# Gates between the pairs of a recurrence, prompt scores on quarter tiles, and later side work in a planned transformer layer

## The chip, the cores and the metric

The kernel runs on one core of one Trainium2 chip. The metric is the time of one execution in device microseconds. A difference is measured by running the two kernels in turn on the same chip. Names used below: PE is the matrix engine (TensorE), DVE the vector engine, ACT the scalar engine, POOL the general engine (GpSimd), SP the engine that issues most DMAs. "Records" are instructions as the profile counts them: an f32 matmul leaves two, an fp32r matmul one.

## The reference, cut to what matters

One layer over 640 tokens (512 prompt tokens and 8 x 16 sample tokens), width 1024, all in f32:

```python
x += 0.5 * swiglu(rms_norm(x), w_ffn1_up, w_ffn1_down)      # d_ff = 2816
h  = rms_norm(x); P = h @ w_in                              # q, k, v, four HGRN blocks, two LRU blocks, 3 gates
A  = sliding-window attention, 16 query heads, 4 key heads of 64, chunks of 64 that see 3 chunks of keys,
     q and k normalised per head, softmax with a learned sink per head
B  = HGRN2: gated linear recurrence with a 128x128 state per head, 8 heads
C  = causal convolution (4 taps), then RG-LRU (a scan over time), times gelu(gate branch)
x += (sig(gA) * A @ w_attn_o + sig(gB) * B @ w_hgrn_o + sig(gC) * C @ w_lru_o) @ w_out
x += 0.5 * swiglu(rms_norm(x), w_ffn2_up, w_ffn2_down)
```

## The kernel before

All activations lie transposed, 128 features on the partitions and the 640 tokens along the row. A projection, `proj`, is one 128-column block of a weight matrix against all tokens: the block is loaded into `wr`, split into a rounded high half `wh` (a cast, L750) and a low half `wl` (a subtraction on DVE, L751), and multiplied in fp32r as three products (`wh` with the high and the low half of the tokens, `wl` with the high half), in two halves of 320 tokens in two banks of the tag `pp` (four banks). With K = 1024 that is 48 matmuls of 320 columns. `halves` pairs the two banks with the halves of a destination. `scaled` empties them while multiplying by `RS`, the row norm's factor per token; with `late` it copies first and multiplies afterwards in one product of 640. `parts` splits a result into high (ACT) and low (DVE) halves for a following projection.

From the fifth FFN block on, `pair` computes a gate block and an up block together from seven products instead of eight (a Strassen form), which needs sums and differences of the normalised tokens. `combos` makes these: a first part at once, and a second part, `rest()`, before the first down projections. `CHUNKS` cuts the 22 FFN blocks in four groups (4, 6, 6, 6), each followed by eight down projections.

In attention, `query(m)` normalises two query heads (one block of 128 features). For the prompt it used to be written into `qb` as a block diagonal (`qb` is 1024 wide, half of it zeros), so that one matmul of K = 128, M = 128 gives the scores of both heads for one chunk of 64 queries. `prompt(m, g, qb)` goes through the chunks in two halves `hh` of four chunks; each half has two score operations, one for each bank `ps` of the tag `me` (two banks in all), each followed by the maximum, the exponentials and the division, then transposes and, by `pv_of`, the product with the values. `sample` does the same for the sample tokens, `merge` multiplies by the output weights and the gates. `AHEAD` tells how many gate projections are put behind each query block.

The LRU, `lru()`, goes through eight feature blocks in four pairs. For a pair: the convolution (DVE), the two small gate matrices (into `me`), exponentials and square roots on ACT, the scan (L1227), and the projections LG with gelu, product and `parts`. After all four pairs five gate projections (`gate(GC, m, "mgC")`) and the first HGRN head's projections follow, then `merge`. The last columns of the convolution and of the scan are copied into `CB` for the outputs.

The order of instructions is not written by hand. Every operation goes into `Sched` with a cost for each engine that may do it, its reads and writes, and a priority: the running number of the projection (`S.item`), plus `S.late`, or minus a `lag` for preparation that may come earlier. `Sched.run` plays the program through with these costs: again and again it takes the operation that can start first, among those within 0.04 us the one of lowest priority, and so fixes each engine's order. Buffers of one tag (and so the banks of `pp` and `me`) are given out in program order. On the chip each engine then follows its fixed order and waits on semaphores. Costs are formulas such as these:

```python
def dve(n, f, aps=0):
    return ("DVE", 0.066 + 1.042e-3 * n + 0.063 * aps, f)
...
return {32: 0.021 + 0.415e-3 * m.n, 64: max(0.112, 0.93e-3 * m.n)}.get(w, max(0.216, 0.011 + m.n / 600.0))
```

Of the kernel before, what the change touches and what calls it, by code (L numbers as in the profile page):

```python
# [16 lines left out]
P = 128  # L17
TP = 512
# [327 lines left out]
def trunk_kernel(ctx: ExitStack, tc: tile.TileContext, A: dict, O: list):  # L346
# [122 lines left out]
    SK = fixed("SK", [P, 32])  # L469
    NAR = 13864  # L470
# [52 lines left out]
    in_region(RW, 2, [("qb", 1024, 2), ("pw", 1024, 2)])  # L523
# [367 lines left out]
    def ffn(wu, wd, norm, R, H, sfx, done, aside=()):  # L891
        ops = None
        for f0, nf in CHUNKS:
            for f in range(nf):
# [16 lines left out]
            if f0 == 0:  # L911
                rest()
            for m in range(KD):
# [58 lines left out]
    def attention():  # L972
        ck, cv = A["cache_attn_k"][0], A["cache_attn_v"][0]
        sk = A["attn_sinks"][0].rearrange("(m two) -> two m", two=2)
        for h in range(2):
            dma(SK[h * 64:h * 64 + 64, 0:8].at(h), sk[h:h + 1, :].to_broadcast([64, 8]), after=(PRM.v,), small=True)
            for b in range(4):
                p0 = b * 32 + h * 16
                dma(SK[p0:p0 + 16, 8:16].at((b, h)), sk[h:h + 1, :].to_broadcast([16, 8]), after=(PRM.v,), small=True)
        S.op([dve(16, lambda: nc.vector.tensor_scalar(SK[:, 16:32](), SK[:, 0:16](), -1.0, None, op0=ALU.mult))], [SK.v, RS.v], [SK.v])  # L980
# [13 lines left out]
        for b in qbs + qss + pws:  # L994
            fill(b.v, 0.0, only=("POOL",))

        def qknorm(ps):
            q, s, r, u = scaled("qq", ps), S.buf("qt"), S.buf("qr"), S.buf("qu")
# [5 lines left out]
        for j in range(2):  # L1004
            q, r = qknorm(proj(W, 0, KD, AK + j * P, RA))
# [35 lines left out]
        def prompt(m, g, qb):  # L1041
            pT = S.buf("pT")
            for hh in range(2):
# [4 lines left out]
                for i in range(2):  # L1048
                    ps = S.buf("me")
                    calls = []  # L1050
                    for c in (2 * i, 2 * i + 1):
                        n = hh * 4 + c
                        w = min(n + 1, 3) * 64
                        o = (c % 2) * 192
                        e = 192 if c % 2 == 0 else 256
                        win[c] = ps[:, o:o + w], pw3[:, c, e - w:e].at(c)
                        calls.append((win[c][0], qb[:, n * P:(n + 1) * P], kd[g][:, (n + 1) * 64 - w:(n + 1) * 64], True, True))
                    mm(calls)
                    if hh == 0 and i == 0:
                        red = [(mx[:, c:c + 1].at(i), win[c][0]) for c in range(2)]  # L1060
# [5 lines left out]
                    ts(mi, mi, -0.125, ALU.mult, SK[:, 16 + m:17 + m], ALU.min, only=("DVE",))  # L1066
                    fn(ei, mi, AF.Exp, bias=SK[:, m:m + 1])
                    for c in (2 * i, 2 * i + 1):
                        fn(win[c][1], win[c][0], AF.Exp, scale=0.125, bias=mx[:, c:c + 1].at(i), accum=den[:, c:c + 1].at(i))
                    tt(di, di, ei, ALU.add, only=("DVE",))  # L1070
                    recip(di, di)
                    for c in (2 * i, 2 * i + 1):
                        ts(win[c][1], win[c][1], den[:, c:c + 1].at(i), ALU.mult)
# [8 lines left out]
            def pv_of(k, n):  # L1082

                src = pT[:, k * 512:k * 512 + n * 256].r("p (c h q) -> p c h q", h=2, q=64)
                mm([(po[h * 64:h * 64 + 64, k * P:(k + n) * P].r("p (c q) -> p c q", q=64), V[:, k, g, :], src[:, :, h, :], k == 0, k == 3)
                    for h in range(2)])
# [82 lines left out]
    def lru():  # L1169
        bds = [S.buf("bd") for _ in range(2)]  # L1170
        for b in bds:
            fill(b.v, 0.0)
        for j in range(4):
            xcs, rs, igs, las, lts = [], [], [], [], []
            for i in range(2):
# [16 lines left out]
                cp(CB[:, m, 0:3].at(m), y[:, TP - 3:TP], only=("POOL", "DVE"))  # L1192
                cp(CB[:, m, 3:27].at(m).r("p (b j) -> p b j", b=NB), smp(y.v)[:, :, SB - 3:], only=("POOL", "DVE"))
# [22 lines left out]
            for i in range(2):  # L1216
# [10 lines left out]
                S.op([dve(T, lambda o=hs.v, a=a.v, t=t.v: nc.vector.tensor_tensor_scan(o(), a(), t(), 0.0, op0=ALU.mult, op1=ALU.add))],  # L1227
                     [a.v, t.v], [hs.v])
                cp(CB[:, m, 27:28].at(m), hs[:, TP - 1:TP], only=("POOL", "DVE"))
                cp(CB[:, m, 28:36].at(m), smp(hs.v)[:, :, SB - 1], only=("POOL", "DVE"))  # L1230
                hss.append(hs)
            for i in range(2):
# [4 lines left out]
                parts(RB, m, g.v)  # L1237
        co = S.buf("co")
# [8 lines left out]
        more = lambda m: gate(GC, m, "mgC")  # L1247
        gates = [more(m) for m in range(5)]
# [7 lines left out]
    def hgrn():  # L1256
# [44 lines left out]
        def head(i):  # L1301
# [31 lines left out]
            for h in (2, 4, 8, 16, 32, 64):  # L1333
# [4 lines left out]
                if h < 32:  # L1338
# [149 lines left out]
```

## Time and profile before

| | us |
|---|---|
| median of three runs | 1921.0 (1920.73 to 1923.34) |
| the profiled execution, its own time | 1923.28 |
| span of the profile, first to last instruction | 1921.5 |
| PE busy | 1898.9 (99%) |
| DVE busy | 1389.1 (72%) |
| ACT busy | 735.8 (38%) |
| POOL busy | 44.3 (2%) |
| mean granted clock of PE | 0.996 |

Roughly, FFN1 ends near 460 us, attention runs from there to 712, its merge to 767, the LRU from 767 to 892, gates, LRU merge and HGRN to 1340, HGRN's merge and `w_out` to 1480, FFN2 to the end. Busy times are unions of the instructions' intervals; a matmul's interval is longer than the distance to the next, since matmuls overlap, so distances from start to start are used for what PE's work costs. Idle time of an engine counts only where PE waits for it. In a row of the timeline the square brackets give the engine's idle time before the row and what ended it.

### The profile page before, as it was taken

To read this page: it belongs to the slowest core of one execution; us is meant where nothing else is said; L and a number is where in the kernel's file an instruction comes from. 1 tells how busy PE (TensorE), PEld (TensorE's weight loads), DVE (VectorE), ACT (ScalarE), POOL (GpSimd) and SP (SyncE) were. 2 spreads that over 40 slices of the span, in tenths; PEclk is the share of its full clock that TensorE was granted. 3 is DMA by queue.
4 is the path that set the end of the run, shared out by engine and by line. 5 is a ranking of instruction groups with operands and counts; after the bars stand their busy time and mean duration, and the time that the engine had idled before them with its cause. 6 is when DMAs were issued, how large, how long until landed. Compare 5 with 4: busy or idle time off the path is not lost.

```text
span 1921.5 us, 35215 instructions
## 1 busy us (share of the span) xinstructions
PE 1898.9 (99%) x14654; PEld 1853.0 (96%) x14654; DVE 1389.1 (72%) x2599; ACT 735.8 (38%) x1295; POOL 44.3 (2%) x86
## 2 busy tenths in 40 slices
PE   8999999999999999999999999999999999999999
PEld 8999999999999999999999999999999999999998
DVE  7897685877787773787547778877556978586784
ACT  6343251433478630876002344335112324142340
POOL 2000000000000000020000000000000000000000
PEclk9999999999999999999999999999999999999999
DMA  6232332224321212213222222222322133222322
GB/s 144 66 94 80 93 87 78 75 78 139 102 62 50 62 48 77 61 57 103 77 77 74 84 80 79 79 81 83 122 72 77 56 99 90 87 65 79 99 64 80
DMA packets 303488, 156.89 MB, mean 82 GB/s; under 512 B 21324, under 2 KB 300956, under 8 KB 303328
## 3 DMA queue, kind: packets, MB, share of 16 engines
q1 hardware_dynamic: 302576, 154.58, 27.7%
q8 instruction: 115, 1.88, 0.4%
q0 software_dynamic: 736, 0.06, 0.4%
q14 instruction: 45, 0.37, 0.1%
q10 hardware_dynamic: 16, 0.00, 0.0%
HBM read 143.32 MB, written 10.63 MB: 80 GB/s over the span
## 4 chain that ended last, share of the span: by engine, by line
PE 93%; DVE 4%; ACT 2%; issue 1%; DMA 1%; SPq 0%; ACTq 0%; DVEq 0%
PE pp L438 84%; PE me L438 4%; PE ml L438 3%; PE ml L447 1%; PE me L447 1%; DVE AR L383 1%; ACT AR L393 1%; DVE AR L369 1%; DVE RB L369 0%; DVE AR L1227 0%; ACT L393 0%; DMA RX<-in_x_prompt_dram 0%; DVE wl L751 0%; SPq L417 0%; DVE RA L369 0%
## 5 line engine op out<-in xcount | busy, mean ns | idle before, releaser
L438 PE MATMUL pp<-RA,wh 128*128 128x320 f32 x4192 | 815.0, 314 | 0.3 <-DVE AR L369 0.3
L438 PEld LDWEIGHTS pp<-RA,wh 128*128 128x128 f32 x4192 | 659.1, 189 | 13.1 <-issue 9.7
L438 PE MATMUL pp<-RA,wl 128*128 128x320 f32 x2096 | 490.7, 310 | 4.9 <-DVE wl L751 4.9
L438 PE MATMUL pp<-RB,wh 128*128 128x320 f32 x2016 | 389.0, 310 | 0.9 <-DVE AR L369 0.9
L438 PEld LDWEIGHTS pp<-RA,wl 128*128 128x128 f32 x2096 | 354.7, 188 | 5.9 <-DVE wl L751 5.9
L438 PEld LDWEIGHTS pp<-RB,wh 128*128 128x128 f32 x2016 | 320.4, 188 | 1.5 <-DVE AR L369 1.4
L750 DVE CAST wh<-wr 128x1024 fp32r<-128x1024 f32 (+2 forms) x142 | 89.4, 630 | 237.2 <-PE pp L438 236.5
L438 PE MATMUL pp<-RB,wl 128*128 128x320 f32 x1008 | 241.9, 310 | 1.6 <-DVE wl L751 1.6
L751 DVE TENSOR_TENSOR wl<-wr,wh 128x1024 fp32r<-128x1024 f32 (+2 forms) x196 | 216.7, 1106 | 1.6 <-ACT wh L750 1.0
L836 ACT CAST RW<-AR 128x512 fp32r<-128x512 f32 x180 | 110.4, 621 | 264.9 <-PE pp L438 135.0
L438 PEld LDWEIGHTS pp<-RB,wl 128*128 128x128 f32 x1008 | 172.1, 188 | 1.9 <-DVE wl L751 1.9
L369 DVE TENSOR_TENSOR AR<-AR 128x640 f32<-128x640 f32 (+12 forms) x272 | 140.0, 519 | 28.9 <-ACT AR L393 16.5
L369 DVE TENSOR_TENSOR AR<-pp,AR 128x320 f32<-128x320 f32 x268 | 127.6, 485 | 35.8 <-PE pp L438 32.7
L393 ACT ACTIVATE AR<-AR 128x640 f32<-128x640 f32 (+2 forms) x184 | 110.5, 604 | 96.9 <-DVE AR L369 89.6
L438 PE MATMUL pp<-RX,RW 128*128 128x320 f32 x864 | 138.6, 309 | 0.0
L438 PEld LDWEIGHTS pp<-RX,RW 128*128 128x128 f32 x864 | 129.6, 188 | 0.0
L833 DVE TENSOR_TENSOR RW<-AR,RW 128x512 fp32r<-128x512 f32 x180 | 122.3, 686 | 2.4 <-ACT RW L836 0.9
L393 ACT ACT_TABLE_LOAD x73 | 93.7, 1283 | 2.5 <-PEq L1476 1.4
L402 ACT COPY AR<-me 128x512 f32<-128x512 f32 (+3 forms) x72 | 25.8, 373 | 123.9 <-PE me L447 115.2
L383 DVE SCALAR_TENSOR_TENSOR AR<-pp,AR 128x320 f32<-128x320 f32 x128 | 61.3, 483 | 15.5 <-PE pp L438 15.4
L438 PE MATMUL pp<-RY,RW 128*128 128x320 f32 x432 | 69.2, 309 | 0.0
L750 ACT CAST wh<-wr 128x1024 fp32r<-128x1024 f32 (+1 forms) x54 | 53.7, 994 | 36.9 <-PE pp L438 36.5
(195 smaller groups left out, 1960.7 us busy)
## 6 DMA issues: line engine op xcount, KB each, us to landing
wr<-in_w_in_dram SPq DMA_DIRECT2D x84, 512.0 KB, 3.7
wr<-in_w_ffn_up_dram SPq DMA_DIRECT2D x52, 512.0 KB, 3.8
AR<-in_w_ffn_up_dram SPq DMA_DIRECT2D x36, 512.0 KB, 4.6
wr<-in_w_ffn_down_dram SPq DMA_DIRECT2D x48, 384.0 KB, 3.3
wr<-in_w_ffn_down_dram SPq DMA_DIRECT2D x16, 256.0 KB, 2.8
wr<-in_w_attn_o_dram SPq DMA_DIRECT2D x8, 512.0 KB, 3.7
AR<-in_state_hgrn_dram SPq DMA_DIRECT2D x8, 512.0 KB, 4.7
wr<-in_w_lru_o_dram SPq DMA_DIRECT2D x8, 512.0 KB, 3.8
```

Of the source, the lines that this page charges most:

```text
L369: alts = [dve(out.n, lambda: nc.vector.tensor_tensor(out(), a(), b(), op=op))]
L383: return S.op([dve(out.n, lambda: nc.vector.scalar_tensor_tensor(out(), a(), ap_of(s), b(), op0=op0, op1=op1), isinstance(s, View))], [a, ...
L393: nc.scalar.activation(out(), a(), func, bias=ap_of(bias), scale=ap_of(scale), **kw)
L402: alts = [act(out.n, lambda: nc.scalar.copy(out(), a()), 0, a), dve(out.n * (1.0 if a.in_psum else 0.5), lambda: nc.vector.tensor_copy(out ...
L438: nc.tensor.matmul(o(), l(), m(), start=s, stop=e)
L447: nc.tensor.transpose(o(), i(), d())
L750: S.op([act(nk * P, lambda: nc.scalar.copy(h(), r())), dve(nk * P * 0.5, lambda: nc.vector.tensor_copy(h(), r()))], [r], [h], lag=2)
L751: S.op([dve(nk * P, lambda: nc.vector.tensor_tensor(l(), r(), h().bitcast(F32), op=ALU.subtract))], [r, h], [l], lag=1.5)
L833: S.op([dve(out.n, lambda: nc.vector.tensor_tensor(out(), a(), b(), op=op))], [a, b], [out], lag=lag)
L836: S.op([act(out.n, lambda: nc.scalar.copy(out(), a()))], [a], [out], lag=lag)
```

## The change

Six edits, and all orders are planned anew.

1. `rest()` gets `S.late = 4.0`, so its operations rank four projections later.
2. In FFN2 the first block's two projections, and in attention the two key projections, use `late` scaling.
3. Prompt scores: `qb` becomes 512 wide without zeros and is written by one product. Each half `hh` has one score operation with eight matmuls of K = 64, M = 64: for each chunk `c` and head `f` the query's 64 features on partitions `b`, the result on partitions `a`. For odd chunks the heads change places in the result, and even chunks go to one `me` bank, odd ones to the other; both banks are taken by the one operation. The sinks SK get eight columns in the changed order, and `pv_of` picks the columns in the changed order.
4. In the LRU a gate projection comes between the two LG projections of each pair.
5. The scan's planned cost goes from `T` to `2 * T`, and a K = 64, M = 64 matmul gets a planned cost of its own.
6. The small copies into `CB`, and those into `hatt` in HGRN, may no longer go to POOL; they go to ACT or DVE.

```diff
+            if l.proto.shape[0] == 64 and w == 64:
+                return max(0.054, 0.42e-3 * m.n)
...
-    in_region(RW, 2, [("qb", 1024, 2), ("pw", 1024, 2)])
+    in_region(RW, 2, [("qb", 512, 2), ("pw", 1024, 2)])
...
-                    late = not sfx and f < 2
+                    late = f < (1 if sfx else 2)
...
             if f0 == 0:
+                S.late = 4.0
                 rest()
+                S.late = 0.0
...
+            dma(SK[64 - h * 64:128 - h * 64, 32:40].at((h, 8)), sk[h:h + 1, :].to_broadcast([64, 8]), after=(PRM.v,), small=True)
...
-            q, r = qknorm(proj(W, 0, KD, AK + j * P, RA))
+            q, r = qknorm(proj(W, 0, KD, AK + j * P, RA), True)
...
-                for i in range(2):
-                    ps = S.buf("me")
-                    calls = []
-                    for c in (2 * i, 2 * i + 1):
...
-                        calls.append((win[c][0], qb[:, n * P:(n + 1) * P], kd[g][:, (n + 1) * 64 - w:(n + 1) * 64], True, True))
-                    mm(calls)
+                pss, calls = [S.buf("me") for _ in range(2)], []
+                for c in range(4):
...
+                    win[c] = pss[c % 2][:, o:o + w], pw3[:, c, e - w:e].at(c)
+                    for f in range(2):
+                        a, b = f * 64, (f ^ (c % 2)) * 64
+                        calls.append((win[c][0][a:a + 64, :], qb[b:b + 64, n * 64:(n + 1) * 64], kd[g][b:b + 64, (n + 1) * 64 - w:(n + 1) * 64],
+                                      True, True))
+                mm(calls)
...
+            stt(qb.v, q[:, 0:TP], prm(QN), r[:, 0:TP], ALU.mult, ALU.mult)
             for h in range(2):
                 a, b = h * 64, h * 64 + 64
-                stt(qb[a:b, :].at(h).r("p (n h q) -> p n h q", n=8, h=2)[:, :, h, :], q[a:b, 0:TP].r("p (n q) -> p n q", n=8), prm(QN, a, b),
-                    r[a:b, 0:TP].r("p (n q) -> p n q", n=8), ALU.mult, ALU.mult)
...
+        gates, more = [], lambda m: gate(GC, m, "mgC")
...
-                cp(CB[:, m, 0:3].at(m), y[:, TP - 3:TP], only=("POOL", "DVE"))
+                cp(CB[:, m, 0:3].at(m), y[:, TP - 3:TP], only=("ACT", "DVE"))
...
-                S.op([dve(T, lambda o=hs.v, a=a.v, t=t.v: nc.vector.tensor_tensor_scan(o(), a(), t(), 0.0, op0=ALU.mult, op1=ALU.add))],
+                S.op([dve(2 * T, lambda o=hs.v, a=a.v, t=t.v: nc.vector.tensor_tensor_scan(o(), a(), t(), 0.0, op0=ALU.mult, op1=ALU.add))],
...
+                if i == 0:
+                    gates.append(more(len(gates)))
...
-        gates = [more(m) for m in range(5)]
+        while len(gates) < 5:
+            gates.append(more(len(gates)))
...
-                            cp(a4[p, :, p].at(j), atc[p, :].r("p (t l) -> p t l", t=NT), only=("ACT", "POOL"))
+                            cp(a4[p, :, p].at(j), atc[p, :].r("p (t l) -> p t l", t=NT), only=("ACT", "DVE"))
```

More of the change, by code (lines that the diff above doesn't have):

```diff
@@ L468, in trunk_kernel @@
     CB = fixed("CB", [P, KD, 36])
-    SK = fixed("SK", [P, 32])
-    NAR = 13864
+    SK = fixed("SK", [P, 48])
+    NAR = 13824
     AR = sb("AR", [P, NAR])
@@ L993, in attention, with qknorm @@
         qbs, qss, pws = ([S.buf(t) for _ in range(2)] for t in ("qb", "qs", "pw"))
-        for b in qbs + qss + pws:
+        for b in qss + pws:
             fill(b.v, 0.0, only=("POOL",))
-        def qknorm(ps):
-            q, s, r, u = scaled("qq", ps), S.buf("qt"), S.buf("qr"), S.buf("qu")
+        def qknorm(ps, late=False):
+            q, s, r, u = scaled("qq", ps, late), S.buf("qt"), S.buf("qr"), S.buf("qu")
             rnorm(q, s, r, u, bd64, 64)
@@ L1047, in prompt @@
                 win = {}
[L1048 to L1060 removed]
+                pss, calls = [S.buf("me") for _ in range(2)], []
+                for c in range(4):
+                    n = hh * 4 + c
+                    w = min(n + 1, 3) * 64
+                    o = (c // 2) * 192
+                    e = 192 if c % 2 == 0 else 256
+                    win[c] = pss[c % 2][:, o:o + w], pw3[:, c, e - w:e].at(c)
[4 more added lines that the diff above has]
+                mm(calls)
+                for i, ps in enumerate(pss):
+                    cols = [(2 * i, win[i]), (2 * i + 1, win[i + 2])]
+                    if hh == 0:
+                        red = [(mx[:, c:c + 1].at(i), v[0]) for c, v in cols]
                     else:
@@ L1065, in prompt @@
                     mi, di, ei = (x[:, 2 * i:2 * i + 2].at(i) for x in (mx, den, es))
[L1066 to L1069, printed above, removed]
+                    pos, neg = ((0, 16), (32, 40))[i]
+                    ts(mi, mi, -0.125, ALU.mult, SK[:, neg + m:neg + m + 1], ALU.min, only=("DVE",))
+                    fn(ei, mi, AF.Exp, bias=SK[:, pos + m:pos + m + 1])
+                    for c, v in cols:
+                        fn(v[1], v[0], AF.Exp, scale=0.125, bias=mx[:, c:c + 1].at(i), accum=den[:, c:c + 1].at(i))
                     tt(di, di, ei, ALU.add, only=("DVE",))
                     recip(di, di)
-                    for c in (2 * i, 2 * i + 1):
-                        ts(win[c][1], win[c][1], den[:, c:c + 1].at(i), ALU.mult)
+                    for c, v in cols:
+                        ts(v[1], v[1], den[:, c:c + 1].at(i), ALU.mult)
                 for i in range(2):
@@ L1191, in lru @@
                     stt(smp(xc.v)[:, :, :s], hist, w, smp(xc.v)[:, :, :s], ALU.mult, ALU.add)
-                cp(CB[:, m, 0:3].at(m), y[:, TP - 3:TP], only=("POOL", "DVE"))
-                cp(CB[:, m, 3:27].at(m).r("p (b j) -> p b j", b=NB), smp(y.v)[:, :, SB - 3:], only=("POOL", "DVE"))
+                cp(CB[:, m, 0:3].at(m), y[:, TP - 3:TP], only=("ACT", "DVE"))
+                cp(CB[:, m, 3:27].at(m).r("p (b j) -> p b j", b=NB), smp(y.v)[:, :, SB - 3:], only=("ACT", "DVE"))
                 r, ig = S.buf("lr"), S.buf("li")
@@ L1226, in lru @@
                 hs = rs[i]
-                S.op([dve(T, lambda o=hs.v, a=a.v, t=t.v: nc.vector.tensor_tensor_scan(o(), a(), t(), 0.0, op0=ALU.mult, op1=ALU.add))],
+                S.op([dve(2 * T, lambda o=hs.v, a=a.v, t=t.v: nc.vector.tensor_tensor_scan(o(), a(), t(), 0.0, op0=ALU.mult, op1=ALU.add))],
                      [a.v, t.v], [hs.v])
-                cp(CB[:, m, 27:28].at(m), hs[:, TP - 1:TP], only=("POOL", "DVE"))
-                cp(CB[:, m, 28:36].at(m), smp(hs.v)[:, :, SB - 1], only=("POOL", "DVE"))
+                cp(CB[:, m, 27:28].at(m), hs[:, TP - 1:TP], only=("ACT", "DVE"))
+                cp(CB[:, m, 28:36].at(m), smp(hs.v)[:, :, SB - 1], only=("ACT", "DVE"))
                 hss.append(hs)
@@ L1246, in lru @@
         dma(O[11], co[28:36, :])
-        more = lambda m: gate(GC, m, "mgC")
-        gates = [more(m) for m in range(5)]
+        while len(gates) < 5:
+            gates.append(more(len(gates)))
         pre.append(heads(0))
```

10 lines of the change are left out of this document (6 added, 4 removed).

## The prediction

> **What bounds the kernel now.** I read the page first, then who TensorE (PE) waits for, then busy times by stretch, then the timeline at each place where PE stands still.
>
> ```profile
> PE 1898.9 (99%) x14654; PEld 1853.0 (96%) x14654; DVE 1389.1 (72%) x2599; ACT 735.8 (38%) x1295; POOL 44.3 (2%) x86
> ```
>
> PE is busy 99% of the span, so only two things can pay: less PE work, or the little that PE stands still or runs slowly. The list of PE's own waits shows how little that is (total us, times, longest):
>
> ```profile
> PE pp L438 <- DVE wl L751: 6.4, 5, 2.4
> PE me L447 <- DMA RX<-in_x_prompt_dram: 4.6, 2, 2.6
> ```
>
> The DMA line is the start, which the change leaves alone. The other is VectorE (DVE) being late with the low half `wl` of a weight block. What follows such a gap costs too. Busy times by stretch (PE, PEld, DVE, ACT, POOL with counts; granted clock, DMA share, GB/s):
>
> ```profile
> 1340.00:1480.00 140.00, 140.00 (x957) 140.00 (x956) 80.94 (x116) 24.70 (x34) 0.00 (x0) 1.00 0.31 95
> ```
> ```profile
> 76.00:86.00 10.00, 8.41 (x46) 7.99 (x45) 9.11 (x21) 3.15 (x5) 0.00 (x0) 0.83 0.19 54
> 780.00:802.00 22.00, 19.22 (x110) 18.33 (x109) 19.73 (x38) 18.07 (x25) 3.72 (x4) 0.84 0.18 53
> 820.00:834.00 14.00, 11.57 (x77) 11.04 (x76) 14.00 (x29) 5.19 (x7) 4.05 (x6) 1.00 0.26 75
> 862.00:868.00 6.00, 5.55 (x35) 4.87 (x34) 6.00 (x14) 2.62 (x4) 2.63 (x3) 1.00 0.23 68
> 1486.00:1492.00 6.00, 5.11 (x33) 4.63 (x32) 4.55 (x8) 0.74 (x1) 0.00 (x0) 1.00 0.00 0
> 1532.00:1542.00 10.00, 8.28 (x45) 7.88 (x44) 8.47 (x15) 1.47 (x3) 0.00 (x0) 0.83 0.16 47
> ```
>
> The first row is undisturbed: 140 us / 957 = 0.1463 us per matmul of 320 columns. Nearly all matmuls of the other stretches are of that kind, so what each lost is its length less its count times 0.1463: 10 - 6.73 = 3.27 (end of the first four FFN1 blocks), 22 - 16.09 = 5.91, 14 - 11.27 = 2.73 and 6 - 5.12 = 0.88 (all LRU, 9.5 together), 6 - 4.83 = 1.17 and 10 - 6.58 = 3.42 (start of FFN2). Sum 17.4 us. Where the clock reads 0.83 or 0.84, matmuls after the gap ran at half speed, so those gaps cost about twice their length.
>
> **The change part by part.** *Combinations later.* The first FFN1 gap in the timeline (start, us, ..., idle before it and its releaser):
>
> ```profile
> 74.90 0.82 DVE L369 TENSOR_TENSOR RA<-AR,RA 128x640 fp32r<-128x640 f32 x1
> ...
> 77.50 0.82 DVE L369 TENSOR_TENSOR RW<-RW 128x640 f32<-128x640 f32 x1
> ...
> 78.23 0.68 DVE L751 TENSOR_TENSOR wl<-wr,wh 128x512 fp32r<-128x512 f32 x1
> ...
> 78.84 0.82 DVE L369 TENSOR_TENSOR RB<-AR,RB 128x640 fp32r<-128x640 f32 x1
> 78.97 0.56 PE L438 MATMUL pp<-RB,wl 128*128 128x320 f32 x2 [1.59 <-DVE wl L751]
> ```
>
> Three operations of `rest()`, 0.82 us each (first and last shown, 2.46 us), stand ahead of the `wl` for which PE waits 1.59. With `S.late = 4` they rank behind it, so `wl` is up to 2.46 us earlier and the gap closes. Next late is the last block's low half in RB, at 78.84; the second down projection has three blocks that don't need it (3 x 6 matmuls, 2.6 us), so I leave 0.4 of the 3.27: gain 2.9. `rest()` then costs eight casts on ACT and ten DVE operations during the down projections, where its first reader is 28 us away (8 x 4 x 6 x 0.1463); I cost it at nothing. Without that cover it would cost its DVE time, 10 x 0.82 = 8.2. FFN2 has the same pattern:
>
> ```profile
> 1535.25 0.82 DVE L369 TENSOR_TENSOR RW<-RW 128x640 f32<-128x640 f32 x1
> ```
> ```profile
> 1536.72 0.56 PE L438 MATMUL pp<-RA,wl 128*128 128x320 f32 x2 [1.72 <-DVE wl L751]
> ```
>
> Gain 3.0 of 3.42.
>
> *Two first projections scaled late.* FFN2's first pair and the two key projections leave PSUM by a plain copy, and RS is applied afterwards.
>
> ```profile
> 1488.49 1.68 DVE L369 TENSOR_TENSOR AR<-pp,RS 128x320 f32<-128x320 f32 x4
> 1489.03 1.11 PE L438 MATMUL pp<-RB,wh 128*128 128x320 f32 x4 [0.89 <-DVE AR L369]
> ```
> ```profile
> 470.25 0.71 PE L438 MATMUL pp<-RA,wh 128*128 128x320 f32 x3 [0.29 <-DVE AR L369]
> ```
>
> PE waited for a `pp` bank that the product with RS had not emptied. Copies need no RS: gains 1.0 of 1.17, and 0.3. Added are eight copies out of PSUM and four products of 640 in place of eight of 320, on engines that are idle there (DVE 4.55 of 6, ACT 0.74 of 6 in the row above).
>
> *Gates between pairs, scan time, copies.* In the LRU stage:
>
> ```profile
> 794.72 0.64 PE L438 MATMUL me<-NL,BH 128*128 128x320 f32 x1 [2.41 <-DVE NL L369]
> ```
> ```profile
> 817.01 1.48 DVE L1227 TENSOR_TENSOR_SCAN AR<-AR 128x640 f32<-128x640 f32 x1
> ```
> ```profile
> 825.37 0.56 PE L438 MATMUL pp<-RA,wl 128*128 128x320 f32 x2 [2.38 <-DVE wl L751]
> ```
> ```profile
> sum 125.00, PE 119.34 PEld 116.90 DVE 99.20 ACT 101.68 POOL 18.32; mean PE 29.83 PEld 29.22 DVE 24.80 ACT 25.42 POOL 4.58
> ```
> ```profile
> L393 ACT ACT_TABLE_LOAD x73 | 93.7, 1283 | 2.5 <-PEq L1476 1.4
> ```
> ```profile
> L393 ACT ACTIVATE AR<-AR,SK 128x2 f32<-128x2 f32 x40 | 10.9, 292 | 11.7 <-DVE AR L377 11.4
> ```
>
> The planner books a scan at T (0.73 us by its formula); the chip takes 1.48, so DVE is late behind each of the eight. The new 2T books 1.40. Four gates, each 48 x 0.1463 = 7.0 us of PE work needing no LRU result, come between the projections of each pair. PE work is only moved: the stage, 125 us from 767 to 892 (the row with the sum), grows to about 153. To DVE a gate adds two products (0.42 each by the 1.68 of four above) and a `wl` of twice the 0.68 above, 2.2 us, four of them 9: 108 of 153. To ACT it adds at most two table loads (2.6 us) and a sigmoid and a cast, which I put as high as the loads: four gates 21, 123 of 153 before the copies. Behind a gate's products on DVE stands the next `wl`, and the following LG projection on PE waits for both; the gate's own 7 us cover that. Gain 7.5 of 9.5; ends 0 and 9.5. The copies into CB leave POOL, where nobody waits for them before the last transposes: no gain. On ACT, 32 copies at no more than the 0.29 of the two-column row are 9 us in the 153, beside PE, and the sixteen of `hatt` lie in a stage where PE never stops. I take 0; all on the path they would cost 9, and below 0 there is nothing, as no one waited for them.
>
> *Prompt scores on 64x64 tiles.* Now, in the timeline, the scores of the second half of a query block:
>
> ```profile
> 633.84 1.57 PE L438 MATMUL me<-AR,RW 128*128 128x192 f32 x8
> 635.11 0.88 PE L438 MATMUL pp<-RA,wh 128*128 128x320 f32 x4
> 635.83 0.45 PE L438 MATMUL pp<-RA,wl 128*128 128x320 f32 x2
> ```
> ```profile
> 602.88 1.26 PE L438 MATMUL me<-AR,RW 128*128 128x64 f32 x8
> 603.84 0.89 PE L438 MATMUL pp<-RA,wh 128*128 128x320 f32 x4
> ```
>
> From start to start, eight records of 192 columns take 1.27 (0.83 ns a column), and the four behind them 0.72 instead of 4 x 0.1463 = 0.59: 1.40 with the switch. The first half takes 0.96 and as much switch: 1.10. Eight blocks: 20.0, and 1.2 more because nine of the halves are split by other work: 21.2 us. New are twice the records, each a quarter of the array. How tiles run side by side is seen in the nearest rows:
>
> ```profile
> 600.72 1.73 PE L438 MATMUL ml<-AR 128*64 128x256 f32 x16
> 602.38 0.66 PE L447 MATMUL ml<-ident,AR 128*128 128x128 f32 x4
> ```
> ```profile
> L438 PE MATMUL ml<-AR 128*128 128x128 f32 x144 | 22.5, 274 | 0.0
> ```
> ```profile
> L438 PE MATMUL me<-AR 128*32 128x128 f32 x128 | 5.2, 279 | 0.0
> ```
> ```profile
> L438 PE MATMUL me<-AR 128*32 128x32 f32 x320 | 4.5, 199 | 0.0
> ```
>
> Two column tiles: four key tiles of 256, 256, 256 and 128 columns, two records and two halves each, are 3584 columns in 1.66 us against 2.96 one by one, a ratio of 0.56. Four column tiles: 5.2/128 us a record against 22.5/144, 0.26. Four 64x64 tiles then take 0.26 to 0.31 (0.56 squared) of what the new records would take singly: (64 + 128 + 6 x 192) x 4 = 5376 columns, 4.46 us a block. That is 1.16 to 1.38. Sixteen switches in and out at about 0.2 (0.13 on the one side above) add 3.2. New sum 12.5 to 14.2, gain 7.0 to 8.7; I take 8. If only two tiles ran at once (0.56), it is 23.2: a loss of 2. One by one, 38.9: a loss of 17.7. In the last row above 320 records take 14 ns each, so no record has a fixed cost that would bind at 16 per half. The Trainium skill's page "TensorE: Matmul & The Clock Gate" (section "Wait — 56ns, not 53.3ns?") says the opposite: starts at least 25 ns apart, and 62 ns if the sequencer decodes each. By 62 ns a half would take 1.0, the gain some 2 us; the 14 ns speak against it.
>
> DVE work also falls: one product of 512 columns for two on 64 partitions. DVE isn't the bound there:
>
> ```profile
> 515.00:712.00 197.00, 196.45 (x1588) 182.51 (x1587) 155.76 (x428) 134.68 (x338) 1.28 (x6) 1.00 0.20 56
> ```
>
> so 0, as are one reduction more per block, the eight SK columns with their two small loads on POOL's queue at the kernel's start, and the two fills of `qb` that go from the same queue.
>
> *Sum.* 2.9 + 3.0 + 1.3 + 7.5 + 8.0 = 22.7. The whole order is planned anew, so new gaps will come; I allow 2.7 for them, somewhat less than what was lost at 1535. Net -20. The profiled execution took 1923.3 (span 1921.5), so 1903.3; the median of the runs is 1921.0, 2.3 lower, and the forecast goes with it: **1901**.
>
> **The rivals.** (a) *Tiles don't overlap fourfold*, for whatever cause, two at a time at best: 10 of the gain go, 1911. For: no row shows a 64x64 tile with f32. Against: the 0.26 and 0.56. (b) *The LRU stage stays bound by DVE and ACT latency*: gates fill PE but ACT (81% busy now) with more table loads makes `wl` late again: 7.5 go, 1908.5. For: ACT is busy 18.07 of 22 us at the worst gap. (c) *The new plan has as many gaps as it cures*, so the change doesn't do what it says outside the scores: 1921 - 8 = 1913. (d) *Slower*: the score operation now takes both `me` buffers at once. If PE comes to it and has to wait until the second is read out, it stands still with every projection behind it in its queue. Priced at PE's wait of 2.41 in the LRU row, sixteen of them are 38 us: 1901 + 38 = 1939. From 1.5 us each (24 in all) it is slower than before. Against: the planner knows of both buffers and fills with projections, and PE is busy 196.45 of 197 us there now. (e) *A fixed issue time per record* takes most of the score gain: at the price at which 16 records equal the old 1.27 (79 ns each) the gain is gone and the switches cost 2, 1911; the row shows 14 ns.
>
> **How the numbers follow.** Forecast as told 0.62; (a) 0.08; (b) 0.11; (c) 0.12; (d) 0.05; (e) 0.02. A change of 0.2% (3.8 us) is about what a measurement of this kernel can tell from none. All but (d) lie below 1917 and are faster; of their 0.95 I leave 0.06 to mixtures of (a) to (c) that end near 1921; 0.05 is slower. With all stalls gone (17.7) and the tiles at 0.26 (8.7) it is 1921 - 26.4 = 1894.6, and I set the low end just below. (a), (b) and (c) reach from 1908 to 1913: the range goes to 1912.
>
> **What would show it.** The score records in `me` as 64*64, twice as many, a half in under 0.9 us; if near 1.3, (a) or (e). No PE wait over 1 us for `wl` near 77 and near 1515 to 1525; clock 1.00 there. Sigmoids of `mgC` between the gelus, and LRU stretches without a PE wait of 2.4; if PE still waits there for `NL` or `wl`, (b). PE waits before `me` scores of 1 us and more: (d). Waits in new places summing to over 10 us: (c) and a wrong forecast.

## The result, and the profile after

The changed kernel takes 1901.0 us (median of four runs, 1900.5 to 1901.2) against 1921.4 for the kernel before on the same chip: ratio 0.9892, 95% interval 0.9875 to 0.9909. The forecast was 1901 (1894 to 1912). The sum came out, but several of its terms did not, and one of them, edit 1, failed; the experiments show how.

The page after, first row (busy us, share of the span, instructions):

```profile
PE 1883.9 (99%) x14782; PEld 1834.8 (97%) x14782; DVE 1388.0 (73%) x2608; ACT 753.9 (40%) x1337; POOL 19.8 (1%) x44
```

PE is busy 15.0 us less, and the span is 23.6 shorter (1897.9). The list of PE's waits in the changed kernel (total us, times, longest):

```profile
PE me L449 <- DMA RX<-in_x_prompt_dram: 4.6, 2, 2.6
PE ml L449 <- DMA AR<-in_norm_ffn_dram: 2.3, 1, 2.3
PE pp L440 <- DVE AR L383: 2.0, 4, 0.6
PE me L449 <- issue: 0.5, 1, 0.5
PE pp L440 <- DVE wl L753: 0.3, 1, 0.3
```

Of the 6.4 us for `wl` 0.3 is left, and the 2.4 for `NL` are gone. New is 2.0 us for L383, the residual product that empties a `pp` bank after a down projection.

Where the time went is found by lining up the starts of the same projection matmul in both traces (their order is the same in every kernel here). The two profiled executions differ by stage as follows (after less before, us):

| stage | difference |
|---|---|
| start, first four FFN1 blocks | -1.15 |
| FFN1's first eight down projections (edit 1) | -1.68 |
| key projections (edit 2) | -0.58 |
| attention and its merge (edit 3) | -7.1 |
| LRU with its five gates (edits 4, 5, 6) | -9.9 |
| FFN2's first pair (edit 2), next blocks | -1.05, -0.36 |
| FFN2's first eight down projections (edit 1) | -1.69 |
| all else | under 0.1 each |

The LRU stage, by stretch (columns as in the prediction):

```profile
757.00:891.00 134.00, 134.00 (x913) 133.44 (x912) 102.94 (x197) 105.03 (x150) 0.16 (x1) 1.00 0.24 70
```

PE stands still nowhere in these 134 us; DVE is busy for 103 and ACT for 105 of them. A score half, in PE's timeline: the second half, then the first half of a later block.

```profile
517.46 0.46 PE L440 MATMUL pp<-RA,wl 128*128 128x320 f32 x2
517.85 0.88 PE L440 MATMUL me<-AR,RW 64*64 64x192 f32 x16
518.66 0.85 PE L440 MATMUL pp<-RA,wh 128*128 128x320 f32 x4
519.36 0.46 PE L440 MATMUL pp<-RA,wl 128*128 128x320 f32 x2
...
609.93 0.77 PE L440 MATMUL me<-AR,RW 64*64 64x64 f32 x16
610.63 0.85 PE L440 MATMUL pp<-RA,wh 128*128 128x320 f32 x4
```

From start to start a half takes 0.81 and 0.70 us. The two `wl` matmuls ahead take 0.39 instead of 2 x 0.1463 = 0.29, and the four `wh` behind 0.70 instead of 0.59: a switch costs 0.1 on each side. Eight blocks: 8 x 1.51 + 16 x 0.2 = 15.3 us, where the old halves came to 21.2.

Last, what is left at FFN1's first down projections, PE and then DVE, and the longest of the waits in FFN2:

```profile
80.79 0.41 PE L440 MATMUL pp<-RB,wh 128*128 128x320 f32 x1 [0.50 <-DVE AR L383]
81.79 0.71 PE L440 MATMUL pp<-RB,wh 128*128 128x320 f32 x3 [0.58 <-DVE AR L383]
```
```profile
76.95 0.82 DVE L369 TENSOR_TENSOR RW<-RW 128x640 f32<-128x640 f32 x1
...
79.03 0.82 DVE L369 TENSOR_TENSOR RA<-RW,RA 128x640 fp32r<-128x640 f32 x1
...
80.25 0.48 DVE L383 SCALAR_TENSOR_TENSOR AR<-pp,AR 128x320 f32<-128x320 f32 x1
```
```profile
1518.87 0.71 PE L440 MATMUL pp<-RA,wh 128*128 128x320 f32 x3 [0.59 <-DVE AR L383]
```

`wl` is now in time, but operations of `rest()` still stand in DVE's queue at 77 and 79 us, now ahead of the residual product. FFN2 has three short waits: 0.24 for a product of `rest()` (RA, L369), then 0.34 and the 0.59 shown for L383.

### The profile page after: what moved, and what is told of

Read it like the earlier page. It is cut to its first block, busy times and chain, and to the rows that moved or that the text cites. A ratio compares the mean times of both kernels' runs of the same rounds, so it can differ in the third digit from the quotient of the medians.

```text
span 1897.9 us, 35461 instructions
## 1 busy us (share of the span) xinstructions
PE 1883.9 (99%) x14782; PEld 1834.8 (97%) x14782; DVE 1388.0 (73%) x2608; ACT 753.9 (40%) x1337; POOL 19.8 (1%) x44
## 4 chain that ended last, share of the span: by engine, by line
PE 98%; DVE 1%; DMA 0%; issue 0%; ACT 0%; SPq 0%; DVEq 0%; ACTq 0%
PE pp L440 88%; PE me L440 4%; PE ml L440 3%; PE ml L449 1%; PE me L449 1%; DMA RX<-in_x_prompt_dram 0%; DVE RB L369 0%; DVE RA L369 0%; DVE wl L753 0%; DVE AR L369 0%; DVE RW L369 0%; ACT AR L402 0%; SPq L417 0%; DVE wh L752 0%; ACT RA L393 0%
## 5 line engine op out<-in xcount | busy, mean ns | idle before, releaser
L752 DVE CAST wh<-wr 128x1024 fp32r<-128x1024 f32 (+2 forms) x133 | 84.1, 632 | 220.2 <-PE pp L440 217.1
L369 DVE TENSOR_TENSOR AR<-AR 128x640 f32<-128x640 f32 (+12 forms) x272 | 140.0, 519 | 31.4 <-ACT AR L393 23.2
L369 DVE TENSOR_TENSOR AR<-pp,AR 128x320 f32<-128x320 f32 x268 | 127.8, 485 | 35.5 <-PE pp L440 32.4
L752 ACT CAST wh<-wr 128x1024 fp32r<-128x1024 f32 (+2 forms) x63 | 61.9, 983 | 67.1 <-PE pp L440 63.1
L383 DVE SCALAR_TENSOR_TENSOR AR<-pp,AR 128x320 f32<-128x320 f32 x128 | 61.2, 484 | 15.5 <-PE pp L440 15.5
L440 PE MATMUL pp<-RA,RW 128*128 128x320 f32 x432 | 66.3, 309 | 0.0
```

Of the source, the lines that this page charges most:

```text
L369: alts = [dve(out.n, lambda: nc.vector.tensor_tensor(out(), a(), b(), op=op))]
L383: return S.op([dve(out.n, lambda: nc.vector.scalar_tensor_tensor(out(), a(), ap_of(s), b(), op0=op0, op1=op1), isinstance(s, View))], [a, ...
L440: nc.tensor.matmul(o(), l(), m(), start=s, stop=e)
L752: S.op([act(nk * P, lambda: nc.scalar.copy(h(), r())), dve(nk * P * 0.5, lambda: nc.vector.tensor_copy(h(), r()))], [r], [h], lag=2)
```

## The experiments

Theory A: the terms add up, each from the PE work or the PE gap that its edit removes. Theory B: what closed the gaps is that the whole order was planned anew. Four kernels carry one part of the change each, on the kernel before. The code cuts show the lines that matter; `...` stands for lines left out.

**Scores alone (edit 3).**
```diff
-                        calls.append((win[c][0], qb[:, n * P:(n + 1) * P], kd[g][:, (n + 1) * 64 - w:(n + 1) * 64], True, True))
+                        calls.append((win[c][0][a:a + 64, :], qb[b:b + 64, n * 64:(n + 1) * 64], kd[g][b:b + 64, (n + 1) * 64 - w:(n + 1) * 64],
```


> The kernel before with the 64x64 score tiles alone (and their planned cost). Theory A, that the change's parts add up because each removes its own PE work or its own gap: PE spends some 6 us less in the score groups (0.70 and 0.81 us a half instead of about 1.0 and 1.3 with fewer switches), 7 us less in attention and its merge, so 6 to 8 us faster than before, with the gaps near 77, 792, 823 and 1535 still there. Rival B, that the gain is mostly that a new plan happens to have fewer gaps: anything from 0 to 15 us faster, with the old gaps gone or moved.

Measured 1915.6, ratio 0.9967 [0.9954, 0.998], 5.5 us less, just under the 6 to 8 of theory A. In the traces attention and its merge are 7.0 us shorter, the same as in the full change, and the old gaps stand elsewhere. The term is the scores' own.

**Gates and scan time alone (edits 4, 5).**
```diff
+                if i == 0:
+                    gates.append(more(len(gates)))
...
-                S.op([dve(T, ...
+                S.op([dve(2 * T, ...
```


> The kernel before with a gate between the two LG projections of each pair and the scan's planned cost doubled, nothing else. Theory A: the LRU stretch loses its PE waits for NL and wl (2.4 us each) and the slow matmuls behind them, 8 to 10 us faster, all of it between the start of the LRU and the fifth gate. Rival B: not that amount, or elsewhere.

Measured 1912.1, ratio 0.9948 [0.9933, 0.9963], 8.9 us less. The LRU stage is shorter by 9.1 us, as theory A has it. In the other stages the traces differ by at most 0.01, but for the start (0.9) and for two where nothing was changed: the first down projections of FFN1 and FFN2 are 1.55 and 1.53 us shorter, with the same gaps in them. That will matter for edit 1.

**Later combinations and late scaling alone (edits 1, 2).**
```diff
+                S.late = 4.0
                 rest()
+                S.late = 0.0
...
-                    late = not sfx and f < 2
+                    late = f < (1 if sfx else 2)
...
+            q, r = qknorm(proj(W, 0, KD, AK + j * P, RA), True)
```


> The kernel before with rest() four projections later and the two late scalings (FFN2's first pair, the keys). Theory A: 1.7 us less in FFN1's first down projections, 0.6 at the keys, 3.1 at FFN2's start and first down projections: 4.5 to 6 us faster. Rival B: not that amount, or elsewhere.

Measured 1919.5, ratio 0.9986 [0.9976, 0.9996], only 1.5 us less. Theory A's 4.5 to 6 is missed. In the trace edit 2 gave what it should (keys -0.6, FFN2's first pair -1.1), so it is edit 1 that falls short: its two places are 1.7 us shorter each than in the profile of before, and yet the median hardly moves.

**Copies alone (edit 6).**
```diff
-                cp(CB[:, m, 0:3].at(m), y[:, TP - 3:TP], only=("POOL", "DVE"))
+                cp(CB[:, m, 0:3].at(m), y[:, TP - 3:TP], only=("ACT", "DVE"))
...
-                            cp(a4[p, :, p].at(j), atc[p, :].r("p (t l) -> p t l", t=NT), only=("ACT", "POOL"))
+                            cp(a4[p, :, p].at(j), atc[p, :].r("p (t l) -> p t l", t=NT), only=("ACT", "DVE"))
```


> The kernel before with the small copies of CB and hatt moved from POOL to ACT or DVE. Theory A: no PE wait hangs on them, so within 1 us of before. Rival C, that POOL's copies held DVE up (they take 0.7 us for a few columns beside DVE): 2 to 4 us faster, in the LRU stretch.

Measured 1919.0, ratio 0.9984 [0.9975, 0.9993], 2.0 us less; the LRU stage is 2.1 shorter in the trace. The second LRU gap is gone. DVE at that place, the kernel before and then with the copies moved:

```profile
822.38 1.55 DVE L369 TENSOR_TENSOR RB<-AR,RB 128x640 fp32r<-128x640 f32 x2
823.86 0.32 DVE L383 SCALAR_TENSOR_TENSOR AR<-RY,PRM,AR 128x104 f32<-128x104 f32 x1
824.09 1.22 DVE L751 TENSOR_TENSOR wl<-wr,wh 128x1024 fp32r<-128x1024 f32 x1
```
```profile
817.68 1.48 DVE L1227 TENSOR_TENSOR_SCAN AR<-AR 128x640 f32<-128x640 f32 x1
819.08 0.14 DVE L403 COPY CB<-RY 128x3 f32<-128x3 f32 x1
819.13 1.22 DVE L751 TENSOR_TENSOR wl<-wr,wh 128x1024 fp32r<-128x1024 f32 x1
```

The `wl` that PE waited for comes 5 us earlier in DVE's order, straight behind the scan and one small copy. DVE was busy all the way to it before, and its operations are no shorter now (the scan 1.47 and 1.48). So the amount is rival C's, but the cause is not: it is theory B's, a new order, and not POOL's time.

The next three stand on the changed kernel and take one thing back.

**The gates after the pairs again.**
```diff
-                if i == 0:
-                    gates.append(more(len(gates)))
```


> The changed kernel with the five gates taken out of the pairs and issued after all pairs, as before; the scan keeps its planned cost of two passes, and all else of the change stays. Theory A (the gates are cover: they give TensorE 6 to 8 us of work each where the pair's recurrence leaves it nothing, so the two gaps of the stage come back): the kernel takes 6 to 9 us longer than the changed one, 1907 to 1910, with a TensorE wait of over 3 us before a gate product of the pairs (L440 or the 64-wide gate matmuls) again. Theory B (what closed the gaps is the plan that follows from the scan's honest cost, the gates' place adds nothing): 1901 to 1902, no wait over 1 us in the stage.

Measured 1913.6, ratio to the kernel before 0.9956 [0.9941, 0.9971]; the full change has 0.9892, so 12 us are lost, more than the 6 to 9 of theory A. In PE's timeline both old waits are back:

```profile
785.33 0.42 PE L440 MATMUL me<-NL,BH 128*128 128x320 f32 x1 [2.42 <-DVE NL L369]
```
```profile
815.64 0.56 PE L440 MATMUL pp<-RA,wl 128*128 128x320 f32 x2 [2.43 <-DVE wl L753]
```

The LRU stage is 10.8 us longer than in the full change, and so 0.8 longer than in the kernel before, though scan cost and copies are as in the change. Theory A by its mechanism, with waits of 2.4 us where it expected over 3: the gates are the cover, and without them the other two edits together gain nothing.

**The scan booked at one pass.**
```diff
-                S.op([dve(2 * T, ...
+                S.op([dve(T, ...
```


> The changed kernel with the scan's planned cost back at one pass over the 640 columns; the gates stay between the projections of each pair. Theory A (gates are cover, the planned cost only orders VectorE's queue): within 1 us of the changed kernel, 1900.5 to 1902. Theory B (the honest scan cost is what closed the gaps): 1906 to 1910 with a wait of 2 us or more back in the recurrence stage.

Measured 1903.1, ratio 0.9902 [0.9887, 0.9916], about 2 us more than the full change; the LRU stage is 1.7 us longer in the trace. The longest wait in it:

```profile
786.76 0.41 PE L440 MATMUL me<-NL,BH 128*128 128x320 f32 x1 [0.41 <-DVE NL L369]
```

Between the two expectations, far nearer to A's: the honest booking is worth some 2 us beside the gates.

**The small copies back on POOL.**
```diff
-                cp(CB[:, m, 0:3].at(m), y[:, TP - 3:TP], only=("ACT", "DVE"))
+                cp(CB[:, m, 0:3].at(m), y[:, TP - 3:TP], only=("POOL", "DVE"))
```


> The changed kernel with the small copies back as before: those to CB allowed on GpSimd or VectorE, those of the chunk transposes on ScalarE or GpSimd; all else of the change stays. Theory A (what the copies alone brought, 2.0 us by one gap of the recurrence stage less, was that the plan put a weight split of VectorE ahead of work that nothing waited for; with the gates as cover there is no such gap left to close): 1900.5 to 1902, no wait of TensorE over 0.6 us in the recurrence stage. Theory B (GpSimd's copies of 0.3 to 1.0 us hold VectorE or the buffers they read, whatever the plan): 1902.5 to 1904, with VectorE's 128x640 operations longer than 0.82 us where a copy runs.

Measured 1901.2, ratio 0.9895 [0.9878, 0.9913]: the changed kernel's time. Copies on POOL, and DVE's largest group of 640 columns, first in this kernel and then in the changed one:

```profile
L405 POOL COPY CB<-AR 128x1 f32<-128x1 f32 x7 | 6.8, 967 | 139.4 <-issue 80.2 <-DVE AR L1238 58.4 <-ACT wh L752 0.8
```
```profile
L369 DVE TENSOR_TENSOR AR<-AR 128x640 f32<-128x640 f32 x104 | 84.8, 820 | 22.9 <-ACT AR L393 22.6
```
```profile
L369 DVE TENSOR_TENSOR AR<-AR 128x640 f32<-128x640 f32 x104 | 84.9, 820 | 18.8 <-ACT AR L393 18.6
```

One column costs POOL 0.97 us here (0.67 in the kernel before), and DVE does not notice (820 ns in both). No wait of PE in the LRU stage is over 0.2 us. So theory A, and by the medians edit 6 is worth nothing in this company. The traces are a little kinder to it: the LRU stage is 0.9 us longer with the copies on POOL, and all four spans are 1898.9 to 1899.7 against 1897.9 to 1898.6. What lies outside the span, between it and the measured time, is 0.7 us shorter, and why is not traced.

**How the quarter tiles work side by side.** First the order of the chunks, then other tiles.
```diff
-                for c in range(4):
+                for c in (0, 2, 1, 3):
```


> The changed kernel with the eight score matmuls of each half issued in the chunk order 0, 2, 1, 3 instead of 0, 1, 2, 3: the same matmuls on the same quarter tiles, but two chunks in a row now use the same two of the four tiles. Theory A (all four quarter tiles work at once only when neighbours in the queue lie on different ones): halves go from 0.70 and 0.81 us start to start to about 1.2 and 1.4, 16 halves by 0.5 = 8 us, 1905 to 1909. Theory B (the queue runs ahead far enough that the order does not matter, or the halves are set by the switch between weight shapes and the fixed issue times): 0.70 to 0.85 a half, 1900.5 to 1902.

Measured 1901.5, ratio 0.9894 [0.9878, 0.9911], no change. A second half in this order:

```profile
518.57 0.90 PE L440 MATMUL me<-AR,RW 64*64 64x192 f32 x16
519.40 0.85 PE L440 MATMUL pp<-RA,wh 128*128 128x320 f32 x4
```

It takes 0.83 us instead of 0.81. That is theory B's, but it left open whether four tiles work at once or whether something else sets the 0.81.

```diff
-                        a, b = f * 64, (f ^ (c % 2)) * 64
+                        a, b = f * 64, (f ^ (c % 2), f, 0, f)[m % 4] * 64
...
-                mm(calls)
+                mm(calls[0::2] + calls[1::2] if m % 4 == 3 else calls)
```


> The changed kernel with four ways to lay the eight score matmuls of a half on the array, by the query block's number modulo 4 (each a different product, so the attention's values are not those of the reference, their sizes are): 0 as in the change (four tiles), 1 all on the two diagonal tiles, in turns, 2 all from the upper 64 rows, into the two column halves in turns, 3 on the two diagonal tiles, four in a row on each. Theory A (four tiles at work at once set the 0.70 and 0.81 us of a half): the two-tile forms take about twice the time between the switches, 1.2 and 1.4 us, and form 3 more again where the queue is in order. Theory B (two tiles that share no rows are all that ever works at once): form 1 as 0, forms 2 and 3 up to twice. Theory C (a half is 16 issues of a fixed 0.04 to 0.05 us whatever the tiles): all four within 0.05 us of 0.70 and 0.81.

Second halves of forms 0 to 3 in PE's timeline, and last a first half of form 1:

```profile
518.65 0.88 PE L440 MATMUL me<-AR,RW 64*64 64x192 f32 x16
519.46 0.85 PE L440 MATMUL pp<-RA,wh 128*128 128x320 f32 x4
...
546.39 1.52 PE L440 MATMUL me<-AR,RW 64*64 64x192 f32 x16
547.84 0.87 PE L449 MATMUL ml<-ident,RW 128*128 128x128 f32 x6
...
574.65 1.52 PE L440 MATMUL me<-AR,RW 64*64 64x192 f32 x16
576.10 0.85 PE L440 MATMUL pp<-RA,wh 128*128 128x320 f32 x4
...
599.02 2.22 PE L440 MATMUL me<-AR,RW 64*64 64x192 f32 x16
601.17 0.85 PE L440 MATMUL pp<-RA,wh 128*128 128x320 f32 x4
...
536.91 1.20 PE L440 MATMUL me<-AR,RW 64*64 64x64 f32 x16
538.05 0.85 PE L440 MATMUL pp<-RA,wh 128*128 128x320 f32 x4
```

From start to start the second halves take 0.81, 1.45, 1.45 and 2.15 us for eight products of one size (the kernel was timed once, at 1909.9). Theory A; B and C are out. With four tiles each tile does two products, with two tiles four. The difference, 0.64 us, is two products, so one of 192 columns holds its tile for 0.32 us. That is 1.66 ns a column, what the whole array took (0.83 for each of two records), and 0.17 us a half is left over that the tiles do not share.

The first halves, whose products have 64, 128, 192 and 192 columns, test this with no free number. The fullest tile has 320 columns in form 0 and 576 in form 1: 320 x 1.66 ns + 0.17 = 0.70 and 576 x 1.66 ns + 0.17 = 1.13 us; the rows show 0.70 (609.93 in the changed kernel) and 1.14. A fixed time per record would make first and second halves equal, since both have sixteen.

Four products in a row on one tile cost the second half of form 3 another 0.70 us. So the queue does look past a product whose tile is busy, which is why the chunk order did not matter, but not past all that wait here. Two products per tile, one at work and one waiting, fit both patterns (6 x 0.32 + 0.17 = 2.09 against 2.15), and the starts of the single records show it: in form 3 the second tile's first record starts 0.71 us into the half, together with the first tile's third product, and in form 0 four records, one for each tile, start within 20 ns.

**Edit 1 undone.** Then the combinations in two other places.
```diff
-                S.late = 4.0
                 rest()
-                S.late = 0.0
```


> The changed kernel with the remaining combinations of the first block of both FFN layers planned early again; all else of the change stays. Theory A (a wait of 1.8 us for wl comes back in both layers and the waits of 0.4 to 0.9 us for the residual product go, so the stall itself hardly changes; but the long wait is followed by half-speed matmuls in some executions and not in others): median 1901 to 1904, the runs apart by 2 us or more, where the changed kernel's lie within 0.8 us. Theory B (each of the gaps costs about twice its length every time, as the prediction has it): 1906 to 1908 with all runs within 1 us.

Measured 1900.7 (1900.3 to 1901.1), ratio 0.9891 [0.9874, 0.9907], against 0.9892 for the full change: edit 1 is worth nothing that these runs can tell. PE's waits are back where the prediction saw them:

```profile
78.01 0.56 PE L440 MATMUL pp<-RB,wl 128*128 128x320 f32 x2 [1.60 <-DVE wl L753]
78.41 0.90 PE L440 MATMUL pp<-RB,wh 128*128 128x320 f32 x4
...
1515.34 0.56 PE L440 MATMUL pp<-RA,wl 128*128 128x320 f32 x2 [1.86 <-DVE wl L753]
```

The stages are 0.15 and 0.30 us longer than in the changed kernel, no more. Against gaps of 1.60 and 1.86 stand 0.50 and 0.58 in FFN1, and 0.24, 0.34 and 0.59 in FFN2. By the starts of the matmuls the long gaps delay PE by 2.0 and 2.3 us, and the short waits together by 1.6 and 2.0; in FFN1 a small transpose on PE costs 0.25 more where it now stands. No half-speed matmuls follow the long gaps in this trace. Theory B is out; of theory A the stall is right, but the spread that it expected did not come: these runs lie within 0.8 us.

**All ten operations tied behind the second down projection.**
```diff
-            if f0 == 0:
-                S.late = 4.0
-                rest()
-                S.late = 0.0
...
                 for o, p in halves(xk(m), ps):
                     stt(o, p, 0.5, o, ALU.mult, ALU.add)
+                if f0 == 0 and m == 1:
+                    rest((xk(1),))
```


> The changed kernel with the remaining combinations of the first FFN block (both layers) not only planned later but tied to come after the residual product of the second down projection. Theory A (the 1.7 us and 1.2 us that TensorE still waits at 80 and at 1517 us are for two PSUM banks whose residual product stands in VectorE's queue behind those combinations): both waits fall to under 0.5 us together, 1 to 3 us faster than the changed kernel, 1898 to 1900. Theory B (the combinations only move to the start of the second block, whose first gate product waits for them): the sum of waits in the two stages stays at 2 to 3 us, 1900.5 to 1902.5.

Measured 1907.8, ratio 0.9928 [0.9913, 0.9943]: 7 us worse. Both theories missed. PE's waits for L383, and DVE and PE at the worst place:

```profile
PE pp L440 <- DVE AR L383: 6.5, 6, 2.0
```
```profile
90.27 1.55 DVE L369 TENSOR_TENSOR RA<-RW,RA 128x640 fp32r<-128x640 f32 x2
91.74 0.88 DVE L383 SCALAR_TENSOR_TENSOR AR<-pp,AR 128x320 f32<-128x320 f32 x2
```
```profile
92.28 0.70 PE L440 MATMUL pp<-RB,wh 128*128 128x320 f32 x3 [1.99 <-DVE AR L383]
...
94.46 1.27 PE L440 MATMUL pp<-RB,wh 128*128 128x320 f32 x4
```

Ten operations in one go put the residual products off again. Behind the wait four matmuls take 1.27 us, with overlap, instead of 0.75: they run at half speed.

**Only the last of them tied, behind the third and fourth.**
```diff
+                if f0 == 0 and m in (2, 3):
+                    last(3 - m, (xk(m),))
```
`last(q)` is the `t1` part of `rest()`, two operations on DVE for each `q`; it is taken out of `rest()`, whose other operations keep `S.late = 4.0`.

> The changed kernel with only the last two to four of the remaining combinations (those of t1) tied behind the residual products of the third and fourth down projection, where VectorE has idle time, instead of all ten behind the second. Theory A (the waits near 80 and 1517 us are VectorE's backlog, and 1.5 us less of it before 80 us closes them): the waits for the residual product fall from 2.0 us to under 1, 0.5 to 2 us faster than the changed kernel, 1899 to 1900.5. Theory B (VectorE is full to 100 us in the first layer, so what moves there comes back as a wait further on, as it did when all ten moved): 1901 to 1904, waits of 1 us or more between 86 and 95 us.

Measured 1899.4 (1899.1 to 1900.1), ratio 0.9885 [0.987, 0.9899]: the fastest of all. Waits for L383, and the one left in FFN1:

```profile
PE pp L440 <- DVE AR L383: 1.2, 2, 0.6
```
```profile
81.46 0.71 PE L440 MATMUL pp<-RB,wh 128*128 128x320 f32 x3 [0.58 <-DVE AR L383]
```

Against the 1900.7 beside it on the same chip it is 1.3 us better, ranges apart. That is 0.07%, small but real in the trace: against the changed kernel the first down projections are 1.0 us shorter in FFN1 and 1.1 in FFN2. (Another 0.8 us of PE work moves from 103 us to 452 us and is not saved.) Theory A holds by the time, though 1.2 us of waits are left where it expected under 1; no new wait came further on.

## Why the prediction was right, and where it was not

**Edit 1: failed.** It was 5.9 us of the sum; in the full change it is worth nothing by the medians and 0.45 in the traces (0.15 and 0.30, from edit 1 undone). Two steps were wrong. The first is "the gap closes" with 0.4 left for the next thing late, for which the prediction named the last block's low half in RB. What came late next was the residual product, because `rest()` was costed at nothing "during the down projections". There DVE is full: in the changed kernel it is busy for 9.59 of the 10 us from 76 to 86, and for all of 1516 to 1520 in FFN2. The prediction's own row, with 9.11 of 10, was the sign.

```profile
76.00:86.00 10.00, 8.92 (x57) 8.17 (x56) 9.59 (x27) 3.67 (x6) 0.00 (x0) 1.00 0.25 71
1516.00:1520.00 4.00, 3.07 (x18) 2.58 (x18) 4.00 (x9) 0.62 (x1) 0.00 (x0) 1.00 0.06 17
```

The second is "those gaps cost about twice their length", which took one execution for the rule. The same stretch, with the same order of instructions up to there and the same gap, in the kernel with the scores alone, and its FFN2 place behind it:

```profile
76.00:86.00 10.00, 8.41 (x57) 7.99 (x56) 9.72 (x24) 3.15 (x5) 0.00 (x0) 1.00 0.18 54
1526.00:1536.00 10.00, 8.29 (x46) 7.88 (x45) 8.23 (x16) 1.45 (x2) 0.00 (x0) 0.83 0.18 52
```

In FFN1 there are 57 matmuls at a clock of 1.00 where the profile of before shows 46 at 0.83. So of the 3.3 us in the prediction's first row about 1.6 were half-speed matmuls that come in some executions only. The kernels with the gates alone and with the copies alone kept both gaps, at full clock in their traces, and their two stages are only 0.15 us each longer than in the changed kernel. That is also why the traces show 1.7 us at each place and the medians none.

**Edit 2: right.** 1.3 us were predicted, and 1.6 are found in the traces.

**Gates, scan and copies: right in kind, too small.** 7.5 us were predicted, and 9.9 are found in the traces; without the gates' place about 12 us are lost. The 2 us held back of the 9.5 were not lost: PE has no gap left there. ACT shows the step as it was foreseen, a gate's sigmoid (in RW) between the pair's work, and beside it the copies:

```profile
780.99 0.74 ACT L393 ACTIVATE RW<-RW 128x640 f32<-128x640 f32 x1
781.63 0.28 ACT L402 COPY CB<-AR 128x1 f32<-128x1 f32 x2
```

Copies at 0 holds in company; alone they gave 2.0 through a new order, which the step "no one waited for them" could not see.

**Scores: right in kind, 8 predicted, 5.9 by the halves, 7.1 by the stage.** The tiles themselves are at the low end of "0.26 to 0.31": the fullest tile's 0.53 and 0.64 us are 1.17 of a block's 4.46, 0.26. The switches were 0.2 as estimated. Missing was the 0.17 us a half that does not overlap, 2.7 us in sixteen. Summed from start to start over all of PE's records in the stage, the score records go from 17.9 to 12.1 us, and the matmuls between them take 1.3 us less, which the count by halves does not hold in full. The old scores stood in 25 groups and the new ones stand in 16; that fewer changes of shape are the cause is likely but not shown. Alone the scores gave 5.5 by the medians. The fixed issue time of rival (e) is out: sixteen records go in 0.70 us, 44 ns each, and the first halves show that the tiles set even that. The Trainium skill's page "TensorE: Matmul & The Clock Gate" (section "Wait — 56ns, not 53.3ns?") gives 62 ns where the sequencer decodes each matmul; these runs do not show that.

**The sum.** The allowance of 2.7 for new gaps was not needed. In the two traces: 20 forecast, edit 1 2.5 less, scores 0.9 less, edit 2 0.3 more, LRU 2.4 more, the allowance 2.7, and 1.5 at the start and in blocks that nothing touched, 23.5 of the 23.6 seen. The medians are only 20.4 apart. Of the 3.2 us between, 1.85 are that the profiled execution of before, with half-speed stretches at both FFN places, lay above its median, 0.55 that the one of the changed kernel lay below its own, and 0.8 that the time outside the span is longer in the changed kernel (2.6 us against 1.8), which is not traced. So the total was right by errors of both signs, and that it met the median to a tenth of a microsecond is luck.

The four single kernels add up to 17.9 of the 20.4. The missing 2.5 us are within what the intervals of the five ratios allow (about 2 to 3 us each), so no interplay is shown by them. That half-speed stretches make most of the spread of the kernel before fits its twenty runs: the eight with a mean clock of 0.998 or more lie between 1919.0 and 1921.7, the four with 0.996 between 1922.4 and 1923.7. But a long gap need not bring them: edit 1 undone keeps both FFN gaps, and its four runs are within 0.8 us at a clock of 1.00. What decides is not shown.

Rivals: (a) two tiles at a time would have been 1.45 a half, seen only when forced. (b) and (d) did not come: PE has no wait in the LRU stage and none for the scores. (c) came in the two FFN layers only, with 2.2 us of new waits.

## What to carry to other kernels

An engine wait closed by moving other work must be followed to the next consumer on the same queue: if that engine is full in the stretch, the wait only changes its name. Here a few operations moved to where the engine idles did more than all moved at once. Independent matmul work placed inside a latency-bound recurrence paid in full. Its place did most of it; the better booking was worth some 2 us beside it, and nothing without it. Price a stall by its length, and its half-speed aftermath by more than one execution.

## What was not expected of the hardware

Gaps of 1.6 to 1.9 us before a `wl` matmul at the two FFN places are in five kernels' traces (before, scores, gates, copies alone, edit 1 undone), ten in all: three (both of before, the second of the kernel with scores alone) are followed by 13 to 15 matmuls at half speed, 1.5 to 1.8 us more, and seven by at most two slower ones. All five LRU gaps of 2.4 us at the first place (before, scores, copies, later combinations alone, and gates after the pairs) are followed by 11 to 21, in the last two behind a further wait of 0.9. Of the four at the second place two are followed by some 10 and 13 (scores and later combinations alone), and two by none (before, gates after the pairs). So a gap of the same length at the same place, behind the same instructions, is followed by half speed in one execution and not in the next. Where it comes, the granted clock falls to 0.50 for 3.41 us, or for twice that, and matmuls of 320 columns start 0.27 us apart instead of 0.146: in the profile of before from 80.37 to 83.78, from 793.75 to 800.58 and from 1537.86 to 1541.27. The Trainium skill's page "TensorE: Matmul & The Clock Gate" (section "What's actually happening") puts the drop behind a window of about 3.4 us without work that runs freely, not from the kernel's start. The traces agree with the length of the window, 3.41 us, and with chance; they do not agree that a gap must be that long, since 1.59 us were enough at 78.97.

A 64x64 f32 tile ran a column in 1.66 ns, no slower than the full array, four at once, with 0.17 us a group that did not overlap and about 0.1 us on each side for the change of shape. POOL took 0.97 us on average to copy one column of 128 values with the copies back on it (0.67 in the kernel before), where ACT took 0.28 for two in a row.
